# A quarter of each weight slab's low part on GpSimd, and coarse recurrence levels copied block by block on ScalarE

## The chip, the core and the metric

The kernel runs on one core of one Trainium2 chip. The engines are TensorE (PE, matrix products into PSUM), VectorE (DVE, elementwise), ScalarE (ACT, elementwise functions), GpSimd (POOL, elementwise on SBUF) and SyncE (SP, which here issues all loads). Each engine works through its own instructions in order, and waits for the others by semaphores. The metric is the device time of one execution in microseconds; lower is better. The time before is a median of 941.81 us of three runs (940.19 to 946.4).

## What is computed

Two layers of a decoder trunk on one sequence of 256 tokens with 1024 channels, in float32. Each layer projects the normalized input to 7124 columns, feeds four token mixers and four gates from them, sums the gated branches, and ends with a squared-ReLU MLP:

```python
for l in range(DEPTH):                                   # 2
    cmod = (c_act @ ada_w[l] + ada_b[l])[:, None, :]
    sh1, sc1, g1, sh2, sc2, g2 = jnp.split(cmod, 6, axis=-1)
    h = _rmsnorm(x, norm_mix_g[l]) * (1.0 + sc1) + sh1
    z = h @ w_in[l]                                      # (256, 7124)
    za, zb, zc, zd, zg = _split(z, [A_COLS, B_COLS, C_COLS, D_COLS, G_COLS])
    ya = _conv_branch(za, ...)          # causal convolution, 31 taps
    yb = _sparse_attn_branch(zb, positions)
    yc = _gla_branch(zc, ...)           # gated linear recurrence
    yd = _hgrn2_branch(zd, ...)         # gated linear recurrence
    gates = jax.nn.sigmoid(zg).reshape(B_, S_, N_BRANCH, D_)
    merged = jnp.sum(jnp.einsum('bsnw,nwd->bsnd', ys, w_branch_out[l]) * gates, axis=2)
    x = x + g1 * (merged @ w_o[l])
    h = _rmsnorm(x, norm_mlp_g[l]) * (1.0 + sc2) + sh2
    x = x + g2 * (jnp.square(jax.nn.relu(h @ mlp_w1[l])) @ mlp_w2[l])
return _rmsnorm(x, final_g)
```

The recurrence of branches C and D is, with per-channel forget factors, `state = state * f_t + k_t v_t`, `o_t = q_t state`.

## The kernel before

**Weights.** Every weight matrix is streamed as slabs of 128 partitions by up to 1024 float32 columns. PE works in the float32r format, so a slab W is split into a high part `wh` (W rounded to float32r) and a low part `wl` = W - wh, and each product is three matmuls (high x high, high x low, low x high). `do_load` issues the load of a slab into one of 5 buffers called `raw` (in the opening 8 more), on SP's queue. `do_split` lets ACT copy raw to `wh` and then DVE subtract `wl = raw - wh`; that subtraction is the last reader of raw, and the next load into that buffer waits for it. There are 138 split slabs a layer: 58 of the input projection (8 of them, those of branch B in the opening of the layer, have 724 columns), 8 of the branches' projections, 8 of `w_o` and 64 of the MLP. The conditioning (`ada_w`) takes 72 slabs more through the same buffers, which are not split: DVE multiplies raw by the row `crow` in place and sums it. Split parts live in 5 pairs of buffers, 4 more in part of the program.

**Order.** The program is emitted by a planner, `Flow`: a main stream of items for PE in a fixed order (`items`), and generators, called chains, for the smaller work (norms, branches A to D, activations of the MLP). A rough price per instruction (`_Meter`) moves a clock for each engine, and a chain's next step is emitted when by these clocks its inputs are there. What is emitted is each engine's order on the chip. `run` splits slabs ahead of their use, up to 6.5 us by the clocks, while there is room.

**The recurrences.** `linear` works out the scores between key and query positions by levels lv = 0 to 7 of halving blocks of m = 2^lv positions. In each of the levels 0 to 6 PE writes 2 x 256 columns of scores for 128 keys into a pair of PSUM banks (`b2`, of which there are two pairs for all branches), and DVE copies them with `copy_predicated` into `AT` (tile `big`) under `masks[:, lv, :]`, which is 1 where a key is in the first half of its block of 2m and the query in the second. Branches C and D run it once in each layer.

**Masks.** `mask_consts` makes the seven masks on POOL, four instructions a level (a memset, two affine_selects, a cast). The step `transposed` at the start of the first layer emits this chain to its end (`fl.drain(state["masks"])`), ahead of the first split slab.

**POOL otherwise** has the small powers of the norms (`rstd`), a few products in the branches, and in the MLP the square `u_ = r_ * r_` of 256 columns, from which DVE subtracts the high part (`uL`).

Of the kernel before, what the change touches and what calls it, by code (L numbers as in the profile page):

```python
# [23 lines left out]
F32 = mybir.dt.float32  # L24
# [32 lines left out]
# columns of the packed per-channel parameters, per layer  # L57
PC_CONVW, PC_CONVB, PC_LNG, PC_LNB, PC_GATEB, PC_LB = 0, 62, 64, 66, 68, 69
# where the parts of the conditioning, (layer, part), are worked out, and those that the tensor engine does
# [14 lines left out]
# pieces of the input projection: columns, and how many k tiles a slab holds  # L74
# [21 lines left out]
class Flow:  # L96
    """Emission order: a stream of weight slabs for the tensor engine, with chains of smaller work
    woven in between where a rough model of the engines says that their inputs are there."""
# [24 lines left out]
    def arrived(self, ap, t):  # L123
        """a tile that is filled by a DMA which ends at t"""
        name, p0, p1, lo, hi = self.region(ap)
        self.mem[name] = ([(p0, p1, lo, hi, t, "dma")], [])

    def freed(self, ap, t):
        """a tile whose place is free from t on"""
        self.mem[ap.tensor.name] = ([], [(0, 128, 0, 1 << 30, t, "dma")])  # L130
# [58 lines left out]
    def start(self, ch):  # L189
        """when the next step of a chain would start"""  # L190
        return max(ch.t, self.clock[ch.next])
# [16 lines left out]
    def drain(self, ch, until=None):  # L208
        """emits a chain to its end (or until something holds), and what else can go on meanwhile"""
        while not ch.done and not (until and until()):  # L210
            go = [c for c in self.chains if not c.blocked] or self.chains
            self.step(min(go, key=lambda c: self.start(c) + (0.0 if c is ch else 300.0 + PRIO.get(c.name, 0.0))))
# [9 lines left out]
class _Meter:  # L222
# [3 lines left out]
    def __getattr__(self, name):  # L226
# [3 lines left out]
        def call(*args, **kw):  # L230
# [13 lines left out]
            if e == "pe":  # L244
                mv = args[2] if name == "matmul" else args[1]
                if name == "transpose":
                    dur = 107.0
                elif mv.dtype == F32R:
                    dur = n / 2.4 + 2.0
                else:  # L250
                    dur = max(4.0 * n / 2.4, 25.0)
                    if out.shape[0] == 32:
                        dur /= 4.0
                    elif mv.shape[0] == 64:
                        dur /= 2.0
            elif e == "act":
                dur = 50.0 + 0.834 * n + 94.0 * ptr + (42.0 if "accum_out" in kw else 0.0)
                func = kw.get("func", args[2] if len(args) > 2 else None)
                tb = TABLES.get(str(func).split(".")[-1], 0)
                if tb and tb != f.table:  # L260
                    f.table = tb
                    dur += 1283.0
            elif e == "dve":
                per = 0.52 if name in ("tensor_copy", "tensor_scalar", "memset") else 1.042
                dur = 68.0 + per * n + 61.0 * ptr
            else:
                dur = 150.0 + 2.1 * n if name in ("tensor_tensor", "tensor_scalar") else 40.0 + 0.8 * n
                if name == "affine_select":
                    dur = 330.0 + 10.0 * n / out.shape[-1]
                if kw.get("op") == OP.pow:  # L270
                    dur = 300.0 + 165.0 * n
# [6 lines left out]
class _Pool:  # L278
    """a pool whose tiles are short-lived: the model knows when their places are free"""
# [15 lines left out]
class Slab:  # L295
    """A piece of a weight matrix: loaded, and split into two float32r parts when it says so."""
# [10 lines left out]
class Item:  # L307
    """A step of the tensor engine's main stream: the slabs it uses, what emits it, what comes before."""
# [8 lines left out]
def trunk_kernel(ctx, tc, x, c, cT, pos, chan, ada_w, ada_t, w_in, mlp_w1, gla_gate_w,  # L317
# [26 lines left out]
    def mm_take(n):  # L344
        """n banks for the main stream; chains that hold some go on until there are enough"""
        while len(banks) < n:
            fl.step_any()
        return [mm_tile() for _ in range(n)]

    def mm_get():  # L350
        """a bank for a chain"""
# [17 lines left out]
    items = []          # in the order of the tensor engine  # L369
    slabs = []          # in the order of their first use  # L370
# [8 lines left out]
    def spread(start, fill):  # L379
        """puts the items of fill between those from start on, evenly"""  # L380
# [48 lines left out]
    def do_split(i, pool):  # L429
# [13 lines left out]
        wl = pl.tile([P, 1024], F32R, name="wl", tag="wl")  # L443
        fl.freed(wh, free)
# [4 lines left out]
        V.tensor_tensor(s.l, s.raw, s.h.bitcast(F32), op=OP.subtract)  # L449
        raw_free.append(fl.end)  # L450
# [61 lines left out]
    def kslabs(w2d, k0, nk):  # L512
        """rows k0 * 128 ... of a matrix of D columns, 128 at a time"""
# [14 lines left out]
    def tok_part(h, sl, done, t, st, i, bank=None):  # L528
        """a slab's part of h @ its columns for token tile t; done gets the finished PSUM tile"""
# [15 lines left out]
    def tok_chunk(h, sl, done, before=None, only=None):  # L545
        """h @ the columns of sl, tokens on partitions"""
# [14 lines left out]
    def chan_chunk(h, sl, done, before=None, keep=False):  # L561
        """the same with the columns on partitions"""
# [45 lines left out]
    # picks the rows 0, 32, 64 and 96 and adds them up, on every partition  # L608
# [5 lines left out]
    class Vec:  # L614
        """a part of the conditioning: [P, KD] with channels on partitions; for gates a row on every partition"""
# [7 lines left out]
        def fill(self, first=False):  # L623
            """the items that work it out, a tile of channels each"""
# [19 lines left out]
        def finish_on_act(self, k):  # L644
            """one tile of channels of a part of the first norm"""
# [16 lines left out]
        def half(self, c_):  # L662
            """half of it on the tensor engine, as four items"""
# [65 lines left out]
    def rstd_of(mean, n):  # L729
        """mean ** -0.5 on [P, n], the eps being in mean"""  # L730
# [8 lines left out]
    def rms(t, ss):  # L739
        """the reciprocal root mean square of the rows of token tile t"""  # L740
# [3 lines left out]
    def residual(t, ps_of, row, ready, ss):  # L744
        """adds the gated output of a product to token tile t, half by half as it is there"""
# [16 lines left out]
    def norm_chain(t, scale, shift, h, update):  # L762
        """residual update, then RMSNorm of token tile t, transposed, scaled, shifted and split"""
# [21 lines left out]
    def norm_first(scale, shift, h, bank):  # L785
        """the same for both token tiles and without an update, tile of channels by tile of channels"""
# [58 lines left out]
    def tr_split(y, h, t, q):  # L845
        """transposes y, the columns q * 512 ... of token tile t, into the two parts of h"""
# [16 lines left out]
    cst = {}  # L863

    def other_consts():
        """what the mixers need: tables of rotations, bounds of the forget gate, masks"""
# [10 lines left out]
        # lower bounds of the forget gate, [P, layer, tile], and one minus them  # L877
# [71 lines left out]
        # those of the first norm are scaled and shifted in one go  # L949
# [40 lines left out]
    def mask_consts():  # L990
# [5 lines left out]
        masks = consts.tile([P, 7, S], U8, name="masks")  # L996
        mks = zp.tile([P, NT * 704 + 64], F32, name="mks", tag="Z")
        cst.update(masks=masks)
        for lv in range(7):
# [13 lines left out]
    class Mix:  # L1013
# [21 lines left out]
        def b2(self):  # L1035
            """two banks of PSUM; whoever takes them gives them back with free()"""
# [21 lines left out]
        def room(self):  # L1058
            """waits for the place of a pair"""
# [223 lines left out]
        def linear(self, nm, Q, K, F, npair, Qx, F2):  # L1283
            """gated linear recurrence over the whole sequence, by halving blocks.
            Q, K, F: [P, npair * S], channels on partitions; F the forget factors"""
# [22 lines left out]
            # attention with the keys on partitions: [half, t, pair]; a half of the channels has one head  # L1308
            # of each pair, or (C) a pair of heads of its own
# [10 lines left out]
            for lv in range(8):  # L1320
# [34 lines left out]
                ov = AT.rearrange("p (a e) (b two i) -> p a (e b) two i", a=2, two=2, i=m)[:, :, :, 1, :]  # L1355
                dv = ps[:, :, 0:256].rearrange("p a (k i) -> p a k i", i=m)
                mk = cst["masks"][:, lv, :].rearrange("p (k i) -> p k i", i=m)
                # to segments twice as long
# [18 lines left out]
                V.copy_predicated(ov, mk[:, None, :, :].to_broadcast([P, 2, 4 * nb, m]), dv)  # L1377
# [218 lines left out]
    def layer(l):  # L1596
# [17 lines left out]
        else:  # L1614
            # tile after tile of the channels, as the conditioning comes in
# [137 lines left out]
        def w1_tok(g, t, sl):  # L1753
            """columns of the first product for one token tile, tokens on partitions, then transposed"""
# [152 lines left out]
class _Late:  # L1907
    """a pair that is there when it is used"""
# [8 lines left out]
class _Box:  # L1917
    """what comes to be known while the program is emitted"""
# [10 lines left out]
def _layout(inputs):  # L1929
# [7 lines left out]
    # per-channel parameters, channels on partitions  # L1937
# [13 lines left out]
    # the weights, slab after slab as they are loaded  # L1951
# [34 lines left out]
```

## Time and profile before

| | |
|---|---|
| median of three runs | 941.81 us (940.19 to 946.4) |
| span of the profiled execution | 943.6 us |
| PE busy | 897.3 us, 95% |
| DVE busy | 713.9 us, 76% |
| ACT busy | 478.9 us, 51% |
| POOL busy | 110.4 us, 12% |
| read from memory | 194.97 MB, 208 GB/s over the span |

The span runs from the first to the last instruction of the profiled execution, one execution out of several; it is 1.8 us above the median of the timed runs. Busy time is the time in which an engine has an instruction under way; matmuls overlap each other, so their single durations add up to more than PE's busy time. Nearly all instructions carry the line 273, that of the planner's helper, so groups are told apart by the names of their tiles. The stages lie at about 0 to 52 us (opening), to 350 us (mixers and output projection of the first layer), to 495 us (its MLP), to 790 us (mixers of the second layer) and to 944 us (its MLP and the end).

### The profile page before, as it was taken

How to read it: one execution, taken by the hardware profiler on the slowest of the kernel's cores; microseconds unless marked ns; L12 is line 12 of the kernel's file. 1: busy time of each engine (PE TensorE's matmuls, PEld its weight loads, DVE VectorE, ACT ScalarE, POOL GpSimd, SP SyncE). 2: the span in 40 equal slices, each digit the busy share in tenths (PEclk: the TensorE clock that was granted, in tenths of full speed). 3: DMA queues.
4: the chain of work that ended last, by engine and by line, in shares of the span. 5: the costliest groups of instructions: out<-in, count | busy, mean ns of one | idle time of the engine just before them, and what ended most of it. 6: DMA issues, size and time to landing. Idle time of an engine off the chain costs nothing. (4 is left out here: it accounts for less than half of the span.)

```text
span 943.6 us, 14391 instructions
## 1 busy us (share of the span) xinstructions
PE 897.3 (95%) x5320; PEld 753.0 (80%) x5320; DVE 713.9 (76%) x1204; ACT 478.9 (51%) x787; POOL 110.4 (12%) x158
## 2 busy tenths in 40 slices
PE   1699999999999999999999999999999999999996
PEld 1699766767778899998978887777777889999995
DVE  7989788787767878888776988887876784555553
ACT  6474754324454544444575567333455564544451
POOL 6800010101000001111110001021000001111110
PEclk9899999999999999999999999999999999999998
DMA  8878545465644598999954554445655456666641
GB/s 315 307 253 284 188 152 179 163 194 179 230 144 158 194 312 322 316 316 315 323 192 174 168 180 155 137 151 158 223 166 172 153 183 221 225 210 216 219 158 46
DMA packets 55558, 196.96 MB, mean 209 GB/s; under 512 B 6432, under 2 KB 6848, under 8 KB 55488
## 3 DMA queue, kind: packets, MB, share of 16 engines
q1 hardware_dynamic: 55488, 196.04, 61.8%
q8 instruction: 42, 0.69, 0.3%
q14 instruction: 28, 0.23, 0.1%
HBM read 194.97 MB, written 1.05 MB: 208 GB/s over the span
## 5 line engine op out<-in xcount | busy, mean ns | idle before, releaser
L273 DVE TENSOR_TENSOR wl<-raw,wh 128x1024 fp32r<-128x1024 f32 (+1 forms) x276 | 329.3, 1219 | 64.7 <-ACT wh L273 63.5
L273 ACT ACTIVATE wh<-raw 128x1024 fp32r<-128x1024 f32 (+1 forms) x276 | 277.6, 1040 | 129.9 <-DMA raw<-in_mlp_w 73.5
L273 PE MATMUL mm<-wh,hTh 128*128 128x512 f32 (+1 forms) x384 | 155.0, 404 | 8.5 <-ACT wh L273 5.1
L273 PE MATMUL mm<-wl,hTh 128*128 128x512 f32 (+1 forms) x384 | 148.1, 386 | 5.5 <-DVE wl L273 5.4
L273 PE MATMUL mm<-wh,hTl 128*128 128x512 f32 (+1 forms) x384 | 147.7, 385 | 0.0
L273 PE MATMUL mm<-h2h,wl 128*128 128x256 f32 x416 | 117.2, 282 | 0.0
L273 PE MATMUL mm<-h2l,wh 128*128 128x256 f32 x416 | 117.2, 282 | 0.0
L273 PE MATMUL mm<-h2h,wh 128*128 128x256 f32 x416 | 117.1, 282 | 0.0
L273 PEld LDWEIGHTS mm<-wh,hTh 128*128 128x128 f32 x384 | 73.2, 191 | 37.2 <-issue 11.9
L273 PE MATMUL acc<-wh,uH 128*128 128x512 f32 x256 | 101.7, 397 | 0.0
L273 PE MATMUL acc<-wl,uH 128*128 128x512 f32 x256 | 101.2, 395 | 0.5 <-DVE wl L273 0.5
L273 PE MATMUL acc<-wh,uL 128*128 128x512 f32 x256 | 101.1, 395 | 0.1
L273 DVE SCALAR_TENSOR_TENSOR raw<-raw,crow 128x1024 f32<-128x1024 f32 x72 | 90.8, 1269 | 3.0 <-DMA raw<-in_ada_t 2.7
L273 PEld LDWEIGHTS mm<-wl,hTh 128*128 128x128 f32 x384 | 73.4, 191 | 17.0 <-DVE wl L273 6.6
L273 PEld LDWEIGHTS mm<-wh,hTl 128*128 128x128 f32 x384 | 73.3, 191 | 13.8 <-DVE hTl L273 0.3
L273 PEld LDWEIGHTS mm<-h2h,wh 128*128 128x128 f32 x416 | 78.3, 188 | 1.0
L273 PEld LDWEIGHTS mm<-h2l,wh 128*128 128x128 f32 x416 | 78.3, 188 | 1.1
L273 PEld LDWEIGHTS mm<-h2h,wl 128*128 128x128 f32 x416 | 78.3, 188 | 0.1
L273 PEld LDWEIGHTS acc<-wh,uL 128*128 128x128 f32 x256 | 48.2, 188 | 11.5 <-DVE uL L273 0.5
L273 PEld LDWEIGHTS acc<-wl,uH 128*128 128x128 f32 x256 | 48.2, 188 | 11.0 <-DVE wl L273 1.1
L273 PEld LDWEIGHTS acc<-wh,uH 128*128 128x128 f32 x256 | 48.2, 188 | 9.7
L273 DVE SCALAR_TENSOR_TENSOR ca<-U,chp,ca 128x256 f32<-128x256 f32 x120 | 53.3, 493 | 0.0
(532 smaller groups left out, 1452.7 us busy)
## 6 DMA issues: line engine op xcount, KB each, us to landing
raw<-in_mlp_w SPq DMA_DIRECT2D x128, 512.0 KB, 5.1
raw<-in_w_in SPq DMA_DIRECT2D x100, 512.0 KB, 4.2
raw<-in_ada_t SPq DMA_DIRECT2D x72, 512.0 KB, 5.5
raw<-in_ada_w SPq DMA_DIRECT2D x24, 512.0 KB, 4.2
raw<-in_w_branch_out SPq DMA_DIRECT2D x16, 512.0 KB, 4.2
raw<-in_w_o SPq DMA_DIRECT2D x16, 512.0 KB, 4.2
raw<-in_w_in SPq DMA_DIRECT2D x16, 362.0 KB, 4.3
x<-in_x SPq DMA_DIRECT2D x2, 512.0 KB, 7.6
```

Of the source, the lines that this page charges most:

```text
L273: return fn(*args, **kw)
```

## The change

`do_split` gives the last quarter of a slab's columns (256 of 1024, or 181 of 724) to POOL, which subtracts them as DVE does the first three quarters. The planner's price for such an instruction on POOL goes from 2.1 to 3.0 ns a column. In `linear` the levels 0 to 3 keep the masked copy; the levels 4, 5 and 6 are copied by ACT, block by block (4, 2 and 1 instructions, of 128, 256 and 512 columns on 16, 32 and 64 partitions), and only four masks are made. The rest of the diff takes comments out.

```diff
@@ class _Meter
-                dur = 150.0 + 2.1 * n if name in ("tensor_tensor", "tensor_scalar") else 40.0 + 0.8 * n
+                dur = 150.0 + 3.0 * n if name in ("tensor_tensor", "tensor_scalar") else 40.0 + 0.8 * n
@@ do_split
         wl = pl.tile([P, 1024], F32R, name="wl", tag="wl")
+        n = 1
+        for d in s.shape[1:]:
+            n *= d
+        cut = n * 3 // 4
...
         A.activation(s.h, s.raw, AF.Copy)
-        V.tensor_tensor(s.l, s.raw, s.h.bitcast(F32), op=OP.subtract)
-        raw_free.append(fl.end)
+        raw = s.raw.rearrange("p a b -> p (a b)") if len(s.shape) == 3 else s.raw
+        V.tensor_tensor(wl[:, :cut], raw[:, :cut], wh[:, :cut].bitcast(F32), op=OP.subtract)
+        end = fl.end
+        G.tensor_tensor(wl[:, cut:n], raw[:, cut:n], wh[:, cut:n].bitcast(F32), op=OP.subtract)
+        raw_free.append(max(end, fl.end))
@@ mask_consts
-        masks = consts.tile([P, 7, S], U8, name="masks")
+        masks = consts.tile([P, 4, S], U8, name="masks")
...
-        for lv in range(7):
+        for lv in range(4):
@@ linear
-                V.copy_predicated(ov, mk[:, None, :, :].to_broadcast([P, 2, 4 * nb, m]), dv)
+                if lv < 4:
+                    ov = AT.rearrange("p (a e) (b two i) -> p a (e b) two i", a=2, two=2, i=m)[:, :, :, 1, :]
+                    dv = ps[:, :, 0:256].rearrange("p a (k i) -> p a k i", i=m)
+                    mk = cst["masks"][:, lv, :].rearrange("p (k i) -> p k i", i=m)
+                    V.copy_predicated(ov, mk[:, None, :, :].to_broadcast([P, 2, 4 * nb, m]), dv)
+                else:
+
+                    ov = AT.rearrange("p (a e) (b two i) -> p a e b two i", a=2, two=2, i=m)
+                    dv = ps[:, :, 0:256].rearrange("p a (e b i) -> p a e b i", e=4, i=m)
+                    yield "act"
+                    for b_ in range(nb):
+                        ks = slice(2 * m * b_, 2 * m * b_ + m)
+                        A.activation(ov[ks, :, :, b_, 1, :], dv[ks, :, :, b_, :], AF.Copy)
                 self.free(ps)
```

## Rows read from the trace of the kernel before

**Rows 1.** The page, part 1: busy us, share of span, instructions
```profile
PE 897.3 (95%) x5320; PEld 753.0 (80%) x5320; DVE 713.9 (76%) x1204; ACT 478.9 (51%) x787; POOL 110.4 (12%) x158
```

**Rows 2.** Windows: length, then PE, PEld, DVE, ACT, POOL busy; granted clock, DMA, GB/s
```profile
50.00:100.00 50.00, 50.00 (x352) 45.99 (x351) 46.73 (x103) 30.44 (x51) 1.58 (x3) 1.00 0.79 258
350.00:400.00 50.00, 50.00 (x322) 45.42 (x322) 41.45 (x56) 23.33 (x33) 7.81 (x8) 1.00 0.90 318
400.00:450.00 50.00, 49.82 (x313) 44.66 (x313) 38.70 (x53) 23.50 (x34) 7.82 (x8) 1.00 0.90 315
850.00:900.00 50.00, 50.00 (x332) 45.82 (x331) 25.93 (x32) 22.40 (x34) 5.50 (x9) 1.00 0.65 225
...
22.00:34.00 12.00, 6.39 (x25) 5.59 (x25) 11.90 (x14) 6.36 (x15) 11.32 (x15) 0.86 0.97 378
```

**Rows 3.** Chain that ended last, a piece in the second MLP: start, us, what
```profile
781.89 5.70 PE mm L273 x48
```

**Rows 4.** Waits of PE, first up to 52 us, then from there: us, times, longest
```profile
PE mm L273 <- DVE wl L273: 5.4, 3, 2.6
PE mm L273 <- ACT wh L273: 5.1, 3, 2.6
PE mm L273 <- ACT hTh L273: 1.5, 1, 1.5
...
PE mm L273 <- DVE wl L273: 1.5, 2, 0.8
...
PE acc L273 <- DVE wl L273: 0.5, 2, 0.3
```

**Rows 5.** Stretch 350 to 475 us: SP's and ACT's waits; loads, KB, us to landing
```profile
SPq L417 <- DVE wl L273: 55.6, 44, 2.4
...
ACT wh L273 <- DMA raw<-in_mlp_w: 56.1, 37, 4.2
...
raw<-in_mlp_w SPq DMA_DIRECT2D x44, 512.0 KB, 5.4
raw<-in_ada_t SPq DMA_DIRECT2D x30, 512.0 KB, 5.5
```

**Rows 6.** Timeline in the first MLP: start us, us, engine, instruction [idle before <-releaser]
```profile
379.85 1.22 DVE L273 TENSOR_TENSOR wl<-raw,wh 128x1024 fp32r<-128x1024 f32 x1 [1.33 <-ACT wh L273]
380.17 1.38 POOL L273 TENSOR_TENSOR u__3681<-r__3680 128x256 f32<-128x256 f32 x1 [9.54 <-ACT r__3680 L273]
...
381.51 0.61 POOL L273 TENSOR_TENSOR u__3690<-r__3689 128x256 f32<-128x256 f32 x1
381.58 0.82 DVE L273 TENSOR_TENSOR uL<-u__3681,uH 128x256 fp32r<-128x256 f32 x1 [0.51 <-POOL u__3681 L273]
...
382.32 0.41 DVE L273 TENSOR_TENSOR uL<-u__3690,uH 128x256 fp32r<-128x256 f32 x1
...
432.10 0.50 PE L273 MATMUL acc<-wl,uH 128*128 128x512 f32 x1 [0.18 <-DVE wl L273]
```

**Rows 7.** Timeline in the second MLP, DVE
```profile
801.56 4.62 DVE L273 TENSOR_TENSOR wl<-raw,wh 128x1024 fp32r<-128x1024 f32 x4
```

**Rows 8.** Groups by form, POOL in the second MLP: busy us, mean ns
```profile
L273 POOL TENSOR_TENSOR u__7856<-r__7855 128x256 f32<-128x256 f32 x1 | 0.6, 613 | 0.8 <-ACT r__7855 L273 0.8
```

**Rows 9.** Timeline in the opening, PE and POOL
```profile
22.55 0.44 PE L273 MATMUL mm<-wh,hTh 128*128 128x362 f32 x1 [2.60 <-ACT wh L273]
24.30 0.67 PE L273 MATMUL mm<-wl,hTh 128*128 128x362 f32 x1 [1.31 <-DVE wl L273]
...
33.14 0.40 POOL L273 CAST masks<-mks 128x256 uint8<-128x256 f32 x1
```

**Rows 10.** DVE's masked copy (timeline) and ACT's copy of 512 columns (groups by form)
```profile
205.75 0.72 DVE L273 COPY_PREDICATED big<-masks,b 128x512 f32<-128x512 uint8 x1
...
L273 ACT ACTIVATE qk<-b 128x512 f32<-128x512 f32 x4 | 2.4, 599 | 22.0 <-PE b L273 21.9
```

**Rows 11.** Timeline at the end of branch A, first layer, DVE and PE
```profile
263.01 0.69 DVE L273 TENSOR_TENSOR yslA<-ca,yshA 128x512 fp32r<-128x512 f32 x1 [0.70 <-ACT yshA L273]
...
263.20 0.39 PE L273 MATMUL mm<-wh,yshA 128*128 128x512 f32 x1
```

More of the change, by code (lines that the diff above doesn't have):

```diff
@@ L1354, in linear @@
                 yield "dve"
-                ov = AT.rearrange("p (a e) (b two i) -> p a (e b) two i", a=2, two=2, i=m)[:, :, :, 1, :]
-                dv = ps[:, :, 0:256].rearrange("p a (k i) -> p a k i", i=m)
-                mk = cst["masks"][:, lv, :].rearrange("p (k i) -> p k i", i=m)
                 ns = w // (2 * m)
```

## The prediction, made before the change was run

> **What bounds the kernel now.** I read the page's shares first, then the table by windows, then the chain that ended last and who waits for whom. TensorE (PE) is busy for 95% of the span, VectorE (DVE) for 76%, ScalarE (ACT) for 51%, GpSimd (POOL) for 12% [rows 1]. In the windows PE is busy for 49.8 to 50.0 of each 50 us, in the mixers and in both MLPs [rows 2]. A busy PE could still hide stalls, so I looked at the chain that ended last: in the second layer's MLP 48 products of 256 columns take 5.70 us, group after group, with no other engine between [rows 3]. That is PE's own pace. So DVE time is worth something only where PE waits for it, and the list of PE's waits is short [rows 4]: in the first 52 us 5.4 us for the low parts wl, 5.1 us for wh and 1.5 us for hTh; in the remaining 892 us 2.0 us for wl. The 7.4 us for wl, and some of the wh, is the most that a faster split can give.
>
> One stretch is less safe than it looks: the first layer's MLP, some 145 us from 350 us on. Five raw buffers go round there. The SP queue waits 55.6 us for DVE to release one behind wl, and ACT waits 56.1 us, 37 times, for the load that follows [rows 5]. 74 loads (44 and 30) in the 125 us of that view make 1.69 us each; five buffers make a lap of 8.4 us, of which 5.4 us is issue to landing. At 432.10 us PE waits for a wl [rows 6]: by then the splits have no lead left. Whatever lengthens a lap there reaches PE.
>
> **The change, part by part.** *The low part.* Each of the 276 split slabs keeps three quarters of its subtraction on DVE and gives one quarter to POOL. Back to back a whole one takes 4.62 / 4 = 1.155 us [rows 7], so a quarter is 0.29 us, 80 us over 276 slabs (the 16 slabs of 724 columns give a little less). Nearly all of it lies beside PE's own work and is worth nothing by itself. POOL gets 276 subtractions of 256 (or 181) columns. The nearest rows are its squares u: 0.61 us where DVE is idle [rows 8], 1.38 us where DVE is in a wl at that moment [rows 6]. POOL's total is thus 168 to 381 us, 18 to 40% of the span, beside its 110.4: no bound.
>
> But a slab is now ready, and its raw buffer free, only when both parts have ended, and both start at the end of wh. Before, that is 1.22 us later [rows 6]. After: if the two don't meet, 1.22 - 0.29 = 0.93 us, a gain of 0.29. If POOL waits as in the 1.38 us row, where it ended 0.48 us after the wl (380.17 + 1.38 against 379.85 + 1.22), 0.93 + 0.48 = 1.41 us, 0.19 later than before. If POOL still needs its 1.38 us once DVE has ended, 2.31 us, 1.09 later. I take +0.19: same shape, same partner, and DVE first as there. The meeting has another side: a uL that meets a running POOL product takes 0.82 us, its neighbour that meets none 0.41 [rows 6]. So DVE's next product can lose 0.41 us a slab against the 0.29 saved: +0.12 us.
>
> The Trainium skill ("SBUF — State Buffer", section "Who interferes with whom") says that a DVE instruction with two SBUF inputs and a GpSimd instruction that reads SBUF shut each other out for the whole instruction. The two rows just read agree. By the rule taken strictly a slab costs the pair 1.155 - 0.29 + 0.61 = 1.48 us in turn, 0.32 more than now, 88 us of DVE over 276 slabs; by the rows it is +0.12, 33 us.
>
> *First MLP.* Four of seven slabs there are split, three are conditioning that DVE reduces. The +0.19 counts for 4/7 of the laps, 0.11 us; DVE's +0.12 delays every release; together 0.23 of 8.4 us, 2.7% of 145 us: **+4 us**, all seen by PE once the lead is gone. Bounds: 0.29 less on 4/7 of the laps only restores the lead, worth the few waits there (-1); 1.09 on 4/7 is 0.62 us or 7.4%: +11.
>
> *Second MLP.* DVE is busy for 25.93 of 50 us [rows 2], POOL's u meets nothing (0.61 us) [rows 8]: **0**, both bounds too, since the splits there can run ahead.
>
> *The opening.* All mask work is put into POOL's queue before the first split, so the first quarter stands behind it. Three of the seven levels go; the fourth ends at 33.14 + 0.40 = 33.5 us now [rows 9], and the first four meet the same DVE products as before. The first wl is then whole at 34.0 to 34.9 us (181 columns: 0.43 us, or up to 1.38), where PE started on it at 24.30 after waits of 2.6 for wh and 1.3 for wl [rows 9]. That is 10 us late. But of PE's 12.0 us of waits in this stretch (5.4 + 5.1 + 1.5) 8.1 come after that point, for inputs that do not depend on the first product; PE can now work through them. Left: +2. Against it, DVE, busy for 11.90 of 12 us there [rows 2], saves 0.2 us on each of 8 slabs: -2. I take **0**. Bounds: -2, and +10 if nothing is worked through. These slabs' raw buffers come free late as well, so loads behind them on the SP queue do too; that is in the upper bound.
>
> *Coarse levels.* 12 masked copies of 0.72 us [rows 10] leave DVE: 8.6 us. ACT gets seven copies a recurrence, none larger than 512 columns, 0.60 us [rows 10], so at most 17 us for four recurrences, on an engine that is half idle. The scores' PSUM pair is now released by ACT, which can stand behind a wh that waits for its load, 1.5 us on average where it does (56.1 / 37) [rows 5]; work of the gates' products on PE hides that. Without this cover: 12 x 1.5 = 18 us. Taken: **0**.
>
> *Branch A, first layer.* Its last step yslA starts at 263.01 while PE starts on yshA at 263.20 [rows 11]: no slack. Up to there DVE's balance is 56 slabs (50 of the input projection, 6 of the branches') x 0.12, less 6 copies x 0.72: +2 us, on an engine that is 7% idle at its fullest [rows 2]. I take **+1**, bounds -1 to +5. Behind the last groups of products no slab is left to split: 0.
>
> Sum: 4 + 0 + 0 + 0 + 1 = +5 us. It is made on a profiled execution whose span is 943.6 us; the median of the three timed runs is 941.81, 1.8 lower, so the sum is added to the median: 946.8, **947 us**.
>
> **The rivals.** *The pair takes turns (slower).* In the first MLP a raw buffer's hold grows by POOL's whole product: +11, and branch A pays 3: 956. It decides once the hold grows by some 0.8 us a slab (0.8 x 4/7 / 8.4 x 145 = 8 us, plus A). For it: DVE is busy for 41.45 and 38.70 of 50 us there with 35 split slabs in 100 us (44 in 125); 0.32 more on each is 11 us, 91 of 100, and then every wait grows. Against it: it still fits, and u waited for one product, not for two. The skill's rule named above is what would do this; one meeting at a time, the trace agrees. *The opening is not worked through (slower).* +10 there and +5 elsewhere: 957. For it: the queue order; against it: PE's 8.1 us of later waits. *The engines do not meet (faster).* All waits for wl go (7.4), and half of the 5.1 for wh behind the same buffers: -10, 932. Against it: the masks stand before the first quarter, and rows 6 show the meeting. That the change does nothing is excluded: the cut is made for every split slab, with no condition.
>
> **How the numbers follow.** About 1% (9.4 us) is what a measurement here can tell from no change. The forecast and what lies within 1%: 0.56. The pair in turns: 0.22. The opening: 0.10. Faster by over 1%: 0.12. So faster 0.12, same 0.56, slower 0.32. The range takes in both slower cases and most of the gain, 936 to 960; it leaves out the strongest gain (0.08) and both losses together (0.10).
>
> **What would show it.** In the profile after: wl on DVE at 0.93 us; a wl on POOL of 0.6 us in the second MLP and 1.0 to 1.4 in the first; PE's first wl product at 34 to 35 us, and yet PE past the opening at the time of before; groups of products in the first MLP 3% longer, in the second still 5.70 us. The forecast is wrong if the mixers begin 5 us later than now, if PE waits for wl by more than 15 us in all, or if the second MLP slows too.

## The result, and the profile after

The changed kernel takes 969.72 us (median of four runs, 966.86 to 971.2) where the kernel before took 941.46 in the same comparison: a ratio of 1.0284, with an interval of 1.0253 to 1.0315. It is slower, by 28 us, and the time lies above the predicted range. The profiled execution has a span of 969.0 us against 943.6.

The first thing to read is where along the program the time was lost. The next table cuts each span at the starts of PE's first products of a kind: the first `mm<-hTh,wh` (end of the opening), the first `acc<-wh,mTh` (output projection), the first `mm<-wh,hTh` of the second layer, its first `acc<-wh,mTh`, and PE's last product. It already holds the experiments below, which are built from these parts: "quarter" is the subtraction on POOL, "copies" the coarse copies on ACT with the three masks fewer, "order" the order in which the planner emits.

| kernel (label) | median us | opening | mixers, layer 1 | output projection and MLP 1 | mixers, layer 2 | the rest |
|---|---|---|---|---|---|---|
| before | 941.5 to 944.2 | 52.7 | 227.2 | 213.7 | 232.3 | 209.4 |
| after | 969.72 | 51.9 | 228.8 | 224.9 | 243.6 | 211.7 |
| quarter alone (e1) | 978.28 | 58.3 | 229.2 | 223.9 | 244.9 | 211.8 |
| copies alone (e2) | 942.85 | 50.5 | 227.9 | 211.6 | 233.9 | 209.4 |
| quarter, old order (e3) | 961.94 | 58.6 | 225.6 | 224.2 | 234.2 | 209.8 |
| no quarter, its order (e4) | 955.68 | 52.5 | 230.3 | 211.9 | 239.9 | 210.7 |
| POOL only writes, old order (e5) | 945.55 | 59.3 | 224.8 | 210.6 | 231.1 | 209.4 |
| whole change, old order (e6) | 958.04 | 52.0 | 226.0 | 222.2 | 234.3 | 209.8 |
| e6 and a sixth raw buffer (e7) | 942.67 | 52.0 | 226.2 | 212.0 | 234.0 | 209.7 |
| quarter in MLP 1 only, old order (e8) | 952.90 | 52.5 | 225.5 | 223.3 | 232.3 | 209.4 |
| after and a sixth raw buffer (e11) | 960.04 | 51.9 | 228.8 | 214.2 | 243.7 | 211.8 |
| e3 without the hold of raw (e13) | 955.40 | 59.1 | 224.9 | 219.4 | 232.5 | 209.4 |

Two places lose 11 us each, the first MLP and the second layer's mixers. The opening, which the prediction feared, loses nothing. Each row is one profiled execution: up to the output projection e8 does what the kernel before does, in the same order, and its mixers take 225.5 us against 227.2, so a difference of 2 us in a stage says nothing by itself.

The page, part 1, after, where [rows 1] stood before; DVE is 11 us busier than before, not less:

```profile
PE 907.7 (94%) x5320; PEld 760.0 (78%) x5320; DVE 725.0 (75%) x1192; ACT 489.1 (50%) x815; POOL 441.8 (46%) x422
```

The three costliest groups of DVE before (line, engine, operation, out<-in, shapes, count; then busy us and mean ns):

```profile
L273 DVE TENSOR_TENSOR wl<-raw,wh 128x1024 fp32r<-128x1024 f32 (+1 forms) x276 | 329.3, 1219 | 64.7 <-ACT wh L273 63.5 <-PE mm L273 0.5 <-PE acc L273 0.4
L273 DVE SCALAR_TENSOR_TENSOR raw<-raw,crow 128x1024 f32<-128x1024 f32 x72 | 90.8, 1269 | 3.0 <-DMA raw<-in_ada_t 2.7
L273 DVE SCALAR_TENSOR_TENSOR ca<-U,chp,ca 128x256 f32<-128x256 f32 x120 | 53.3, 493 | 0.0
```

And the same groups after, with POOL's:

```profile
L273 DVE TENSOR_TENSOR wl<-raw,wh 128x768 fp32r<-128x768 f32 (+1 forms) x276 | 312.6, 1153 | 103.8 <-ACT wh L273 103.0 <-PE acc L273 0.4
L273 DVE SCALAR_TENSOR_TENSOR raw<-raw,crow 128x1024 f32<-128x1024 f32 x72 | 100.0, 1396 | 2.5 <-DMA raw<-in_ada_t 2.3
L273 DVE SCALAR_TENSOR_TENSOR ca<-U,chp,ca 128x256 f32<-128x256 f32 x120 | 59.4, 550 | 0.0
...
L273 POOL TENSOR_TENSOR wl<-raw,wh 128x256 fp32r<-128x256 f32 (+1 forms) x276 | 352.6, 1290 | 377.8 <-ACT wh L273 347.5 <-DVE big L273 11.2 <-PE acc L273 9.8
```

A quarter of the columns went, and the mean subtraction on DVE fell by 66 ns of 1219. The conditioning sums (`raw<-raw,crow`) and the convolution (`ca`), which the change doesn't touch, became 10% and 12% longer. 102 of the 276 subtractions on DVE took more than 1.4 us, where 8 did before. The timeline after shows how (start us, us; first POOL, then DVE, from one stretch; then both engines where they start together):

```profile
334.39 3.12 POOL L273 TENSOR_TENSOR wl<-raw,wh 128x256 fp32r<-128x256 f32 x2 [2.83 <-ACT wh L273]
...
334.35 0.96 DVE L273 TENSOR_TENSOR wl<-raw,wh 128x768 fp32r<-128x768 f32 x1 [0.49 <-ACT wh L273]
335.95 0.96 DVE L273 TENSOR_TENSOR wl<-raw,wh 128x768 fp32r<-128x768 f32 x1 [0.65 <-ACT wh L273]
336.83 1.76 DVE L273 SCALAR_TENSOR_TENSOR raw<-raw,crow 128x1024 f32<-128x1024 f32 x1
...
380.29 0.74 POOL L273 TENSOR_TENSOR wl<-raw,wh 128x256 fp32r<-128x256 f32 x1 [2.29 <-ACT wh L273]
...
380.29 1.55 DVE L273 TENSOR_TENSOR wl<-raw,wh 128x768 fp32r<-128x768 f32 x1
```

Where DVE is first it takes 0.96 us and POOL 1.56 (3.12 / 2); where POOL goes through first it takes 0.74 and DVE 1.55. The conditioning sum behind POOL's second part takes 1.76 in place of the 1.21 that it takes where it meets no work of POOL. The engines take turns.

The windows after, to be read against [rows 2] (length; PE, PEld, DVE, ACT, POOL busy; granted clock, which is the share of TensorE's full clock that the chip let it have; DMA share, GB/s):

```profile
350.00:400.00 50.00, 50.00 (x327) 45.69 (x326) 42.16 (x55) 22.98 (x34) 27.98 (x26) 1.00 0.88 311
400.00:450.00 50.00, 48.21 (x299) 43.27 (x298) 40.43 (x54) 21.79 (x32) 24.28 (x24) 0.97 0.87 299
450.00:500.00 50.00, 46.27 (x267) 39.55 (x266) 36.77 (x46) 25.23 (x40) 27.87 (x26) 0.97 0.71 240
500.00:550.00 50.00, 46.15 (x308) 42.43 (x307) 40.25 (x99) 26.70 (x53) 15.93 (x18) 0.97 0.52 170
550.00:600.00 50.00, 46.96 (x289) 35.52 (x287) 42.74 (x87) 33.27 (x62) 16.05 (x15) 0.93 0.41 137
850.00:900.00 50.00, 50.00 (x322) 45.29 (x321) 32.48 (x33) 23.35 (x34) 33.35 (x28) 1.00 0.61 207
...
100.00:150.00 50.00, 44.96 (x264) 31.98 (x262) 44.20 (x84) 30.10 (x61) 15.87 (x14) 0.97 0.43 138
650.00:700.00 50.00, 49.51 (x222) 37.91 (x221) 30.43 (x42) 22.60 (x29) 22.63 (x19) 1.00 0.58 195
```

Two rows of before that [rows 2] does not have:

```profile
100.00:150.00 50.00, 48.84 (x290) 34.74 (x289) 38.27 (x78) 35.46 (x67) 4.39 (x4) 1.00 0.51 168
550.00:600.00 50.00, 50.00 (x317) 38.41 (x317) 41.43 (x79) 34.03 (x65) 5.37 (x6) 1.00 0.52 159
```

PE now stands still in the first MLP (48.21 of 50) and in the first halves of both mixers (44.96, 46.96), where DVE is busy for 43 to 44 us; in the second layer's later mixers DVE idles (30.43, where it was 41.32).

PE is also slower while it works. Its 5320 instructions keep it busy for 907.7 us in place of 897.3. The five rows from 100 to 150 and from 400 to 600 us have granted clocks of 0.93 to 0.97; before, behind the opening and ahead of the end, only one row of 50 us was below 1.00 (250 to 300 us, 0.97). (1 - clock) x 50 adds up to 9.5 us after and 1.5 before, so some 8 of the 28 us are lost by running at the lower of the clock's two levels (1.2 in place of 2.4 GHz); the rest is mostly standing still.

The second MLP has no such loss (50.00 of 50, clock 1.00). Its chain after, as in [rows 3], still has groups of 48 products in 5.70 us:

```profile
807.50 5.70 PE mm L273 x48
```

PE's waits after, up to 52 us and then from there, beside [rows 4] (us in total, times, longest):

```profile
PE mm L273 <- POOL wl L273: 6.1, 1, 6.1
PE mm L273 <- ACT wh L273: 2.6, 1, 2.6
PE mm L273 <- ACT hTh L273: 1.2, 1, 1.2
PE mm L273 <- DVE wl L273: 0.9, 1, 0.9
...
PE acc L273 <- DVE wl L273: 3.4, 4, 1.8
PE b L273 <- DVE big L273: 3.3, 5, 1.0
PE b L273 <- DVE yslB L273: 2.3, 1, 2.3
PE mm L273 <- DVE ynorm L273: 1.9, 1, 1.9
```

In the opening one wait for POOL has taken the place of several; behind it stand waits for `wl`, and new ones for steps of the branches (`big`, `yslB`) and of the norms.

### The profile page after: what moved, and what is told of

The parts are those of the page before. It is cut to its first block, busy times and chain, and to the rows that moved or that the text cites. A ratio compares the mean times of both kernels' runs of the same rounds, so it can differ in the third digit from the quotient of the medians.

```text
span 969.0 us, 15054 instructions
## 1 busy us (share of the span) xinstructions
PE 907.7 (94%) x5320; PEld 760.0 (78%) x5320; DVE 725.0 (75%) x1192; ACT 489.1 (50%) x815; POOL 441.8 (46%) x422
## 5 line engine op out<-in xcount | busy, mean ns | idle before, releaser
L273 POOL TENSOR_TENSOR wl<-raw,wh 128x256 fp32r<-128x256 f32 (+1 forms) x276 | 352.6, 1290 | 377.8 <-ACT wh L273 347.5
L273 DVE TENSOR_TENSOR wl<-raw,wh 128x768 fp32r<-128x768 f32 (+1 forms) x276 | 312.6, 1153 | 103.8 <-ACT wh L273 103.0
L273 PE MATMUL mm<-wh,hTh 128*128 128x512 f32 (+1 forms) x384 | 158.1, 412 | 6.5 <-ACT wh L273 2.6
L273 PEld LDWEIGHTS mm<-wh,hTh 128*128 128x128 f32 x384 | 74.9, 195 | 36.1 <-issue 10.5
L273 DVE SCALAR_TENSOR_TENSOR raw<-raw,crow 128x1024 f32<-128x1024 f32 x72 | 100.0, 1396 | 2.5 <-DMA raw<-in_ada_t 2.3
L273 DVE SCALAR_TENSOR_TENSOR ca<-U,chp,ca 128x256 f32<-128x256 f32 x120 | 59.4, 550 | 0.0
```

The source lines that it names most:

```text
L273: return fn(*args, **kw)
```

## The experiments

The theories are named in the expectations by letters: C, the copies on ACT carry the loss; P, the planner's new order does; L, DVE and POOL meeting at the same slab does. They can hold together, and the runs are made to size each.

**Which part of the change.** e1 is the kernel before with `do_split` and the planner's price from the change; e2 is the changed kernel with the subtraction whole and the old price:

```diff
 e2, do_split of the changed kernel
-        V.tensor_tensor(wl[:, :cut], raw[:, :cut], wh[:, :cut].bitcast(F32), op=OP.subtract)
...
-        G.tensor_tensor(wl[:, cut:n], raw[:, cut:n], wh[:, cut:n].bitcast(F32), op=OP.subtract)
+        V.tensor_tensor(s.l, s.raw, s.h.bitcast(F32), op=OP.subtract)
```

> The kernel before with the quarter on GpSimd and its planner price (3.0 ns a column), but with all masks and masked copies as before. If the loss comes from the quarter (by the planner's order or by the two engines meeting): 965 to 972 us, the whole of the 28 us. If the copies on ScalarE carry a part of it (theory C), this kernel is faster than the changed one by that part: by 5 us or more, 960 or below.

> The changed kernel with each low part whole on VectorE again: only the coarse copies on ScalarE and the three masks less. If the copies are harmless, as the prediction has it: 938 to 944 us. If theory C holds and they carry a part of the loss: 946 or more, with new waits of PE behind ScalarE's copies in the recurrences.

Measured: e1 978.28 us, 1.0371 (1.0345 to 1.0398), above both of its ranges; e2 942.85, 0.9991 (0.9973 to 1.0009). The quarter loses all of it, and more than the whole change. The copies are harmless alone, and beside the quarter they give back 8.6 us (978.28 - 969.72). Most of that is the opening, 58.3 against 51.9: with seven masks ahead of it in POOL's queue the first quarter comes too late to be made up for, with four PE still waits 6.1 us for it but is past the opening no later than before.

**The engines or the order.** A low part is booked by the planner as it is executed, so the quarter also changes what the planner believes of DVE: 0.87 us a slab (68 + 1.042 x 768 ns) where it had booked 1.135 (68 + 1.042 x 1024). e3 executes the quarter and books the whole; e4 executes the whole and books the quarter; e6 is e3 with the copies and the three masks fewer. The instructions of PE, DVE and ACT stand in e3 in the order of before, in e4 in that of e1, in e6 in that of e2.

```diff
 e3
-        V.tensor_tensor(s.l, s.raw, s.h.bitcast(F32), op=OP.subtract)
...
+        fl.note("dve", 68.0 + 1.042 * n, [s.raw, s.h], [s.l])
+        nc.vector.tensor_tensor(wl[:, :cut], raw[:, :cut], wh[:, :cut].bitcast(F32), op=OP.subtract)
+        nc.gpsimd.tensor_tensor(wl[:, cut:n], raw[:, cut:n], wh[:, cut:n].bitcast(F32), op=OP.subtract)
 e4
...
+        fl.note("dve", 68.0 + 1.042 * cut, [raw[:, :cut], wh[:, :cut]], [wl[:, :cut]])
+        end = fl.end
+        fl.note("pool", 150.0 + 3.0 * (n - cut), [raw[:, cut:n], wh[:, cut:n]], [wl[:, cut:n]])
+        nc.vector.tensor_tensor(s.l, s.raw, s.h.bitcast(F32), op=OP.subtract)
+        raw_free.append(max(end, fl.end))
```

> The quarter runs on GpSimd, but the planner books the whole subtraction on VectorE, so that every engine's instructions stand in the order of the kernel before. Theory P (the planner's new order, with VectorE booked too cheaply, makes the mixers' 10 to 16 us each): mixers within 3 us of before, the first MLP still some 10 us longer, 950 to 956 us. Theory L (VectorE and GpSimd meeting on the same slab lengthens VectorE's work, whatever the order): 963 us or more, mixers' first halves as long as in the changed kernel.

> The whole subtraction runs on VectorE, but the planner books it as three quarters there and a quarter on GpSimd, so that the instructions stand in the order of the kernel with the quarter alone. Theory P: slower than before by what the order costs, 10 to 20 us (952 to 962), with waits of PE for chain steps in the first halves of the mixers, and the first MLP as before. Theory L: as before, 939 to 945, since the engines do not meet.

> The whole change, with the planner booking the whole subtraction on VectorE (1.135 us a full slab, where 1.15 was measured with the quarter away): every engine in the order of the kernel with the copies alone. If order and meeting add up, the order's 13 us go and the opening is worked through: 953 to 957 us, first MLP still 10 us longer, second layer's mixers within 4 us of before. If the order is no cause of its own beside the meeting: 965 or more.

Measured: e3 961.94, 1.0200 (1.0171 to 1.0229); e4 955.68, 1.0144 (1.0116 to 1.0172); e6 958.04, 1.0158 (1.0115 to 1.0201; its profiled execution, with a span of 952.4, lies at the fast end of its runs), 1 us above the range that was expected. e3 lies between the ranges of the two theories, and both hold, each for its share: 19 us come from the quarter in the old order, 13 from the order without any meeting. Together they make 32 of e1's 35.6; the other 3 us are within the intervals. e6 takes 11.7 us off the changed kernel by the planner's booking alone (1.0284 to 1.0158 against the kernel before of each comparison). The table shows where: the order costs 7.6 us in the second layer's mixers and 3.1 in the first's, and nothing in the MLP; the quarter in the old order costs 10.5 us in the first MLP, 5.9 in the opening with seven masks, and about 2 in the second mixers, no more than two executions can differ. The 5.9 of the opening are not the engines meeting but the masks ahead of the quarter in POOL's queue, as e5 below shows.

What the order does is seen in e4. Waits of PE from 100 to 165 us, then from 500 to 645 us:

```profile
PE b L273 <- DVE yslB L273: 1.8, 1, 1.8
PE b L273 <- DVE big L273: 1.5, 3, 0.7
...
PE b L273 <- DVE FE L273: 1.5, 1, 1.5
PE mm L273 <- DVE Qd L273: 1.4, 1, 1.4
```

and in its windows from 110 to 130 us, with one of the second layer:

```profile
110.00:120.00 10.00, 8.26 (x40) 4.57 (x38) 9.02 (x20) 7.54 (x17) 3.84 (x4) 1.00 0.56 181
120.00:130.00 10.00, 9.95 (x54) 7.26 (x55) 8.12 (x14) 6.46 (x19) 0.00 (x0) 0.66 0.31 97
...
570.00:580.00 10.00, 7.99 (x58) 5.29 (x56) 9.36 (x18) 8.21 (x12) 0.00 (x0) 1.00 0.71 256
```

Steps of the recurrences and the norms are emitted before their inputs are there, PE takes its queue in order and waits, with main products behind. The wait for `yslB` costs twice: in the row after it the granted clock is 0.66 (1.00 there before), so part of that row runs at 1.2 in place of 2.4 GHz, (1 - 0.66) x 10 = 3.4 us lost beside the 3.3 us of waits of the first stretch. Not every wait does: around those of the second stretch the clock stays at 1.00.

**What passes between the engines.** e5 is e3 with two fills of the quarter, which read nothing (it leaves out the low part of these columns).

```diff
-        nc.gpsimd.tensor_tensor(wl[:, cut:n], raw[:, cut:n], wh[:, cut:n].bitcast(F32), op=OP.subtract)
+        nc.gpsimd.memset(wl[:, cut:n].bitcast(F32), 0.0)
+        nc.gpsimd.memset(wl[:, cut:n].bitcast(F32), 0.0)
```

> As the quarter in the old order (961.94 us), but GpSimd only writes its quarter of each slab, twice with a constant (2 x 0.31 us by the masks' own fills), and reads nothing: the low part of these 256 columns is left out. Theory L in its strict form (the two engines shut each other out while both read SBUF): every wl on VectorE takes 0.95 us, none 1.48; the first MLP comes back to the time of before; only the opening keeps its loss of up to 6 us behind the masks: 942 to 949 us. If a second engine at the slab is what costs (its waits, its release of the buffer), whatever it does: 958 or more.

Measured: 945.55 us, 1.0027 (1.0009 to 1.0045). Groups of e5:

```profile
L455 DVE TENSOR_TENSOR wl<-raw,wh 128x768 fp32r<-128x768 f32 (+1 forms) x276 | 259.9, 954 | 92.7 <-ACT wh L273 70.3 <-POOL wl L457 11.0 <-issue 9.8
L273 DVE SCALAR_TENSOR_TENSOR raw<-raw,crow 128x1024 f32<-128x1024 f32 x72 | 91.0, 1272 | 3.5 <-DMA raw<-in_ada_t 3.3
...
L457 POOL MEMSET wl<- 128x256 f32 (+1 forms) x276 | 86.4, 313 | 15.8
```

DVE's subtraction takes 0.954 us on average, the conditioning sums are back at 1.272, the first MLP at 210.6. The fills do run beside DVE: 110 of the 260 subtractions of 768 columns overlap one, and their median is 0.958 us against 0.957 for the other 150. So it is POOL's reading that makes DVE longer; its writing doesn't. And here is the price of the masks: PE's one wait for POOL in the opening,

```profile
43.31 0.67 PE L273 MATMUL mm<-wl,hTh 128*128 128x362 f32 x1 [15.56 <-POOL wl L457]
```

of which 6.6 us are left at the end of the opening (59.3 against 52.7). Note too that 69 us less of DVE time (329.3 - 259.9) brought at most some 3 us in the first MLP and 1 to 2.4 in the mixers of a layer, hardly more than two executions can differ: there was little to win.

**The first MLP.** e8 has the quarter in the 64 slabs of MLP 1 alone, e7 is e6 with one more raw buffer that the planner doesn't count, e11 the changed kernel with the same, and in e13 POOL subtracts `wh` from itself and so holds no raw (the low part of these columns is left out).

```diff
 e8
...
+        cut = n * 3 // 4 if s.part else n
...
 e7, e11
-    rawp = ctx.enter_context(tc.tile_pool(name="rawp", bufs=NB_RAW))
+    rawp = ctx.enter_context(tc.tile_pool(name="rawp", bufs=NB_RAW + 1))
 e13, from e3
-        nc.gpsimd.tensor_tensor(wl[:, cut:n], raw[:, cut:n], wh[:, cut:n].bitcast(F32), op=OP.subtract)
+        nc.gpsimd.tensor_tensor(wl[:, cut:n], wh[:, cut:n].bitcast(F32), wh[:, cut:n].bitcast(F32), op=OP.subtract)
```

> The kernel before, with the quarter on GpSimd only in the 64 slabs of the first layer's MLP, planner's order as before. If the loss of the first MLP is made there: 951 to 955 us, all of it between the output projection and the second layer, opening and mixers within 2 us of before. If what comes in late from the mixers makes it: 946 or less.

> The kernel with the whole change in the old order, and a sixth raw buffer (the planner still counts five, so the order stays). If the first MLP loses its 10 us because each raw buffer is held longer (the prediction's lap): its stretch comes back to about 214 us from 224, in all 944 to 948. If it loses them because VectorE's own work there has become too long: no gain, 953 to 957.

> The changed kernel in its own order, with a sixth raw buffer that the planner does not count. If order and buffer lap are two separate losses: the first MLP comes back to 211 to 214 us, the mixers keep their 13, in all 953 to 960. If the late mixers come from the same lap: 942 to 947.

> As the quarter in the old order (961.94 us), but GpSimd subtracts the quarter of wh from itself: the same instruction with the same two reads, only that it reads no raw buffer and so holds none (the low part of these columns is left out). If the shutting out alone costs (VectorE's wl and the conditioning sums longer, 1.12 and 1.48 us in the first MLP): 956 to 963 us, the first MLP 6 to 10 us longer than before. If the raw buffer held to GpSimd's end costs (0.24 us a slab beyond VectorE's end): the first MLP comes back by half or more, 948 to 954.

Measured: e8 952.90, 1.0118 (1.0078 to 1.0158), all of it in the MLP's stretch (223.3 against 213.7); e7 942.67, 0.9996 (0.9981 to 1.0012); e11 960.04, 1.0163 (1.0130 to 1.0196); e13 955.40, 1.0129 (1.0095 to 1.0164). A sixth buffer gives the first MLP back whole (212.0 and 214.2), with and without the order's loss, and leaves the mixers as they were, though DVE's subtractions are no shorter in that MLP (mean 1.218 us in e7, 1.159 in e6): the loss there is the lap of the raw buffers, not DVE's load. (Without the quarter the sixth buffer leaves that stage at 210.5 us, in c6 and e12 below, where it was 213.7 and 211.6.) ACT's waits for loads from 350 to 475 us in e6 (us, times, longest):

```profile
ACT wh L273 <- DMA raw<-in_mlp_w: 62.4, 33, 5.0
```

The same row in e7, with the sixth buffer:

```profile
ACT wh L273 <- DMA raw<-in_mlp_w: 37.6, 25, 2.9
```

After the change it was 64.0 (35 times) where [rows 5] had 56.1. Without POOL's hold on raw (e13) about half is left, 219.4 - 213.7 = 5.7 of the 10.5 us. But e13's part on POOL is also shorter (mean 1109 ns against e3's 1232), so it shuts DVE out for less; the split into halves is rough, and 4.8 us (224.2 - 219.4) is the most that the hold can have. Its 955.40 us lie between its two ranges, and e7's 942.67 below its first.

**The order's price.** Is a cheap price bad, or any other order? e9 and e10 are the kernel before with the low part booked at 1.00 and at 1.30 us.

```diff
-        V.tensor_tensor(s.l, s.raw, s.h.bitcast(F32), op=OP.subtract)
...
+        fl.note("dve", 68.0 + 0.91 * n, [s.raw, s.h], [s.l])      # e10: 1.204
+        nc.vector.tensor_tensor(s.l, s.raw, s.h.bitcast(F32), op=OP.subtract)
```

> The kernel before, nothing changed but the planner's price of a low part on VectorE: 1.00 us for a full slab in place of 1.135 (the quarter's order books 0.87, and cost 13 us by itself). If too cheap a price is what makes the order bad: part of that loss, 946 to 953 us, with waits of PE for chain steps in the first halves of the mixers. If any other order is worse or better by chance: 940 or less, or more than the 955.7 of the cheaper price.

> The same with 1.30 us a slab, dearer than measured (1.15 to 1.22). If too cheap a price is what makes the order bad, a dear one costs nothing or little: 939 to 946 us, no waits of PE for chain steps; only the last branch could come late (branch A, 5 us at most). If any change of the order costs: 950 or more, as with the cheap price.

Measured: e9 945.54, 1.0015 (0.9996 to 1.0034); e10 962.37, 1.0182 (1.0153 to 1.0211). So it is not cheapness alone that costs: 1.00 costs nothing to be seen (945.54 lies in neither of its ranges), the dear price costs 18 us, where at most 946 was expected. One part of e10's loss is of the expected kind, at the last step of branch A:

```profile
275.12 0.50 PE L273 MATMUL mm<-wh,yshA 128*128 128x512 f32 x1 [3.81 <-ACT yshA L273]
```

There the chain is emitted late and PE waits for the branch's result. But the larger part of e10's loss is a wait for a step of the recurrences, as in e4 and against the expectation (PE's waits from 52 us on, then two windows):

```profile
PE b L273 <- DVE big L273: 5.2, 5, 2.3
...
140.00:150.00 10.00, 5.99 (x50) 4.24 (x52) 8.92 (x20) 6.83 (x19) 0.00 (x0) 0.65 0.00 0
150.00:160.00 10.00, 10.00 (x59) 6.60 (x57) 6.56 (x13) 3.29 (x5) 0.00 (x0) 0.67 0.33 103
```

In these 20 us PE stands still for 4.0 us, and the clock takes (0.35 + 0.33) x 10 = 6.8 more. In the changed kernel the result of branch A, at 263 us and without slack in [rows 11], is ready 49 us before its use:

```profile
217.32 0.69 DVE L273 TENSOR_TENSOR yslA<-ca,yshA 128x512 fp32r<-128x512 f32 x1 [0.70 <-ACT yshA L273]
...
266.65 0.47 PE L273 MATMUL mm<-wh,yshA 128*128 128x512 f32 x1
```

Prices of 1.00 and 1.135 us serve, with 1.22 measured in the kernel before; 0.87 and 1.30 don't. Four prices don't make a law, and an order can also lose by chance: why 1.30 makes PE wait for `big` is not shown. What is shown is that a booking 23% below the old one (e4, with the quarter booked on POOL beside it) or 15% above it (e10) cost 13 and 18 us with the same work on every engine.

**Six buffers without the quarter.** c6 is the kernel before with the sixth buffer, e12 the copies alone with it.

> The kernel before with the sixth raw buffer alone, nothing else changed. If the buffer is what made the copies with six buffers 0.5% faster than before: 938 to 941 us. If the fewer masks in the opening made a good part of it (their opening was 2.2 us shorter): 941 to 943.

> The copies alone (942.85 us), each low part whole on VectorE, with a sixth raw buffer. The first MLP of this kernel keeps a lead of 0.8 us at its narrowest, so a sixth buffer has little to give: 939 to 943 us. If the splits' lead hides a loss that the waits don't show: 938 or less.

Measured: c6 942.35, 0.9987 (0.9972 to 1.0002); e12 939.75, 0.9950 (0.9931 to 0.9969). e12 is the fastest, 0.5% below the kernel before. Neither the copies nor the buffer makes a difference by itself that can be told, so which of the two gives it stays open.

## Why the prediction was wrong, step by step

**What bounds the kernel.** Right: PE was the bound, and 69 us less on DVE in e5 left the time where it was. The rows shown for it were the fullest, though; in other windows of the mixers PE is busy for as little as 48.3 of 50 us (700 to 750 us). That a bound PE can also be slowed had no place in the sum: what its clock lost behind stalls is some 8 of the 28 us.

**A step that was missing: the planner.** The prediction costed each instruction where it ran and never asked what the planner would do with a lower price, though it books every instruction and its clocks make the order. e4 puts 13 us on that, e6 takes 11.7 us off by it. No rival had it either. The first layer's mixers came out right in time by luck (+1 us said, 228.8 against 227.2 measured): branch A was to be late for want of slack; it was ready 49 us early, and PE waited at steps that the planner had emitted too soon, some 120 us into the program. The second layer's mixers, for which the sum had nothing, lost 11.3 us.

**The low part: mis-sized.** Taken were +0.19 us of hold for a slab and +0.12 of DVE. Over the 64 slabs of MLP 1 the mean from the end of `wh` to the end of the later part went from 1.73 to 2.30 us, +0.57 (from the ends of `wh` and of both parts in the traces). Three things were not in the step. The row it went by [rows 6] had DVE first; where POOL was first, DVE took 1.48 to 1.55 us. DVE is mostly not free when `wh` ends (the mean subtraction starts 0.90 us later, 0.50 before) while POOL mostly starts within 0.1 us, so POOL meets whatever DVE is at, and DVE's other work with two operands pays: the sums by 127 ns on average, the convolution by 57. And POOL's part takes 0.74 us where it goes first, not the 0.61 of the square [rows 8]; the square reads one tile twice, and so does POOL in e13, which took 0.61. DVE's subtractions gave 17 us in place of 80, and the sums and the convolution took 15 back.

The Trainium skill ("SBUF — State Buffer", "Who interferes with whom") has it that a DVE instruction with two inputs in SBUF and a GpSimd one that reads SBUF exclude each other, and that one that only writes doesn't matter. The traces agree on both: 1.48 us for the pair in turn by the prediction's working against 1.48 to 1.56 measured, and e5's 0.954. They do not show that the second stands for all of the first's time: with POOL's own 0.74 in the place of the square's 0.61 the pair in turn would take 0.954 + 0.74 = 1.69 us, more than any row here shows for two that start together.

**First MLP: the mechanism right, the size wrong.** The lap of the raw buffers was the limit, as said; e7 shows it. The term was +4 us with an upper bound of +11; measured 11.2 (224.9 - 213.7), and 9.6 for the quarter there alone (e8). That is the rival in which the pair takes turns, whose +11 for this stretch is the number that came. In part this is luck: its +11 stood on 1.09 us of hold, and with the measured 0.57 the prediction's own lap gives 0.57 x 4/7 / 8.4 x 145 = 5.6 us. The lap from one load into a buffer to the next, taken over all loads of this MLP, went from 8.81 to 9.11 us, 3.4%; what makes up the rest of the 11.2 is not shown. What the prediction held against it, that a square had waited for one product and not two, says how long a meeting is, not how often engines meet when both start at every `wh`.

**Opening: right in time, and mostly by its own reasoning.** PE started the product that needs the quarter at 33.95 us (34 to 35 was said), after a wait of 6.12 us. Its first product with a low part was not late at all (23.84 us against 24.30 before), since the first half of a slab needs no quarter, which the prediction had not seen. PE was past the opening 0.8 us earlier than before. e1 and e3 show the condition: with the seven masks left in front, 5.6 and 5.9 us are not worked through.

```profile
23.84 0.67 PE L273 MATMUL mm<-wl,hTh 128*128 128x362 f32 x1 [0.87 <-DVE wl L273]
...
27.33 0.51 PE L273 MATMUL mm<-wh,hTh 128*128 128x362 f32 x1
33.95 0.67 PE L273 MATMUL mm<-wl,hTh 128*128 128x362 f32 x1 [6.12 <-POOL wl L273]
```

**Coarse levels and the second MLP: right.** e2 is at 0.9991 for the copies; the groups of 48 products still take 5.70 us, and the rest of the program grew by 2.3 us.

The sum as it turned out, from the medians: +19.2 for the quarter in the old order (e3; by the table 5.9 of it the masks ahead of the quarter, the rest the meeting), +13 for the order (e4), about +3.4 for both at once (e1, within the intervals), -8.6 for the masks and copies (e1 to after): 27, where 28 were measured.

## What to carry to other kernels

Where a planner or a hand-made order goes by prices, a change of what an instruction costs is a change of the order too: test the two apart, by executing one and booking the other. Where part of DVE's two-operand work went to GpSimd here and the two ran at the same time, each meeting cost DVE some 0.5 us or GpSimd some 0.8, and DVE paid also on work that was not moved. In a ring of load buffers the time that counts is from a buffer's arrival to its last reader: one more buffer took back all that the quarter lost in the first MLP (e7, e11). Without the quarter it brought nothing that can be told (c6).

## What the runs showed of the hardware

GpSimd's subtraction of 256 columns took 0.74 us where it went first (0.61 in e13, with one tile as both inputs) and 1.5 to 1.56 behind DVE's 0.96; a GpSimd fill of the same columns (0.313 us) left DVE at 0.954. A DVE instruction that came second took about 0.53 to 0.55 us more (0.954 to 1.49, 1.21 to 1.76), less than the 0.74 that GpSimd showed alone. After a stall of PE (1.8 us for `yslB`, 120 us into e4) the granted clock of the row of 10 us that follows was 0.66, so the stall's aftermath cost as much as the waits; a row of the same run in which PE stood still for 2.0 of 10 us (570 to 580 us) kept 1.00.
